# Alternating the row groups of the 32-row inverse products, and splitting a two-bank PSUM tile

## The chip, the cores and the metric

The kernel runs on one core of a Trainium2 chip. The metric is the device time of one launch in microseconds. Five instruction streams run side by side: TensorE (PE, with its weight loads shown apart as PEld), VectorE (DVE), ScalarE (ACT), GpSimd (POOL) and SyncE (SP), which issues DMAs. Each stream is in order, and semaphores join them.

## The reference

One step of a two-layer hybrid decoder over 2064 prompt positions and 8 single-token samples. Each layer projects `x` (1024 channels) to 5128 channels, runs three mixers side by side, projects back and normalises. Two of the mixers matter here.

Retention, per head, runs over the sequence in chunks: scores within the chunk, the old state's contribution, and a new state.

The gated delta rule, per head and chunk of 64 positions, solves a unit lower triangular system and then updates a state:

```
a_low = where(strict, einsum('bhid,bhjd->bhij', kb, k) * decay, 0)
sol   = triangular_solve(eye + a_low, rhs, left_side=True, lower=True)
v_new = u - einsum('bhik,bhkv->bhiv', w, s)
s     = s * exp(g_last) + einsum('bhik,bhiv->bhkv', k * exp(g_last - gc), v_new)
```

The kernel forms the inverse of `eye + a_low` for each chunk and head once, and multiplies by it.

## The kernel before

**Tiling.** Each layer handles the sequence in two halves (`sblock`, 1024 and 1048 columns). A half runs sixteen stages in a written order: keys (K), the RG-LRU heads (A), retention (B) and the delta rule (C). Every stage projects slabs of 128 output channels: `proj` runs 24 matmuls of 128x128 weights on up to 512 columns into a PSUM tile `pj` of one bank. A `Pump` steps generators with the earlier stage's small work between those matmuls.

**The planner.** No engine operation is issued when it is written. `Recorder.note` stores it with its operands; `span` counts PSUM in whole banks over all 128 partitions, so two operations on one bank depend on each other whenever one writes. `places` makes the first users of a pool slot wait for all users of the tile that held it before. `order` then runs a list schedule with fixed costs (a matmul of 32x32 in F32 is put at 0.061 us), taking on each engine, of what is ready, the operation written first; VectorE and ScalarE operations that read PSUM go ahead of others. `issue` emits the operations in that order, and each engine's stream is then fixed; the tile framework adds the semaphores.

**The inverses** (`inverses`). Two chunks of 64 positions lie on partitions 0 to 63 and 64 to 127 of a tile `ap`, for 8 tiles and 4 heads: 32 pairs. Each 64x64 triangle is inverted in 32x32 blocks: `solve` inverts the diagonal blocks on VectorE, and TensorE computes the block below the diagonal, `t21`, by two products of 32x32. They go in two rounds `q` of 16 pairs. The first product (`pg <- tn, ap`) reads rows 0 to 31 for the first chunk and 64 to 95 for the second, and writes partitions 32 to 63 and 96 to 127 of a bank `pg`; VectorE scales it into `gt`, one operation a chunk. The second product (`pg <- tt, gt`) reads rows 32 to 63 and 96 to 127 and writes partitions 0 to 31 and 64 to 95 of another `pg`; ScalarE copies it into `t21`, one copy a chunk. In both products all sixteen of the first chunk come before the sixteen of the second, and in the second product the first chunk's copy is written before the second chunk's products. In the trace a product in F32 shows as two pairs of weight load and matmul. `inverses` runs beside retention or RG-LRU projections, four times in all (two halves, two layers).

**The tile `pz`** is 128 x 1024 F32, two banks, in one slot. In a delta stage (`chain`) four tiles of 128 positions fill it, two tiles to a bank; after them four ScalarE activations and one VectorE multiplication of 64x512 read it into `q.o`. In `retention_bg` the first group of four tiles holds the first bank and the second group the second; `bn_stats` reads each 128 columns as they are finished, and a `tensor_scalar` reads all at the end.

Of the kernel before, what the change touches and what calls it, by code (L numbers as in the profile page):

```python
# [8 lines left out]
F32 = mybir.dt.float32  # L9
F32R = mybir.dt.float32r  # L10
BF = mybir.dt.bfloat16
AF = mybir.ActivationFunctionType
OP = mybir.AluOpType
# [325 lines left out]
def hymba_step(ctx: ExitStack, tc: tile.TileContext, x0t, x0, win, wab, wout, wg, vec, fbc, const, rope,  # L339
# [4 lines left out]
    V, A, PE, G, SP = (Engine(rec, n, e) for n, e in (  # L344
        ("DVE", nc.vector), ("ACT", nc.scalar), ("PE", nc.tensor), ("POOL", nc.gpsimd), ("SP", nc.sync)))
# [5 lines left out]
    psum = Pool(rec, "psum", ctx.enter_context(tc.tile_pool(name="psum", bufs=1, space=PSUM)))  # L351
# [40 lines left out]
    def pt(name="pt"):  # L392
        return psum.tile([128, 512], F32, tag="pt", name=name, bufs=2)
# [2 lines left out]
        return psum.tile([128, 512], F32, tag="pj", name="pj", bufs=2)  # L396

    def pz2():
        return psum.tile([128, 1024], F32, tag="pz", name="pz", bufs=1)

    def p1(tag):
        return psum.tile([128, 512], F32, tag=tag, name=tag, bufs=1)
# [147 lines left out]
    def layer(l):  # L550
# [42 lines left out]
        def sblock(sb):  # L593
# [79 lines left out]
            egw = eg[:, 4].rearrange("p (t h) -> p t h", h=4)  # L673
            egc = eg[:, 0].rearrange("p (t h) -> p t h", h=4)
# [149 lines left out]
            def inverses():  # L824
                nf = nb2.rearrange("p t h -> p (t h)")
                pn = pt("pn")
                PE.transpose(pn[:32, :128], nf[:, :32], ident)
                nbs = small("nbs", [128, 32])
                for c in range(4):
                    A.copy(nbs[32 * c:32 * c + 32], pn[:32, 32 * c:32 * c + 32])  # L830
                a_ = wk.tile([128, 32, 32], F32, tag="q", name="as_", bufs=2)
                apf = ap.rearrange("p t h i -> p i (t h)")
                for c in range(4):
                    o = 32 * (c % 2)
                    V.transpose(out=a_[32 * c:32 * c + 32], in_=apf[32 * c:32 * c + 32, o:o + 32])

                yield
                yield from solve(a_, nbs, t21, tt.rearrange("p s i -> p (s i)"), 128, 32)
                V.transpose(out=tt.rearrange("p s i -> p i s"), in_=t21)
                tn = big("v", "tn")[:, :1024].rearrange("p (s c) -> p s c", c=32)  # L840
                V.transpose(out=tn, in_=tt)
                yield
                yield
                for q in range(2):
                    s = slice(16 * q, 16 * q + 16)
                    pg = pt("pg").rearrange("p (s c) -> p s c", c=32)
                    gt = wk.tile([128, 16, 32], F32, tag="gm2", name="gt", bufs=1)
                    for c in range(2):
                        o = 64 * c
                        for k in range(16):  # L850
                            t, h = divmod(16 * q + k, 4)
                            PE.matmul(pg[o + 32:o + 64, k], ap[o:o + 32, t, h, 32:64], tn[o:o + 32, 16 * q + k],
                                      start=True, stop=True)
                    for c in range(2):
                        o = 64 * c + 32
                        V.tensor_tensor(gt[o:o + 32], pg[o:o + 32],
                                        nf[o:o + 32, s].unsqueeze(2).to_broadcast([32, 16, 32]), op=OP.mult)
                    yield
                    pg = pt("pg").rearrange("p (s c) -> p s c", c=32)
                    for c in range(2):  # L860
                        o = 64 * c + 32
                        for k in range(16):
                            PE.matmul(pg[o - 32:o, k], gt[o:o + 32, k], tt[o:o + 32, 16 * q + k],
                                      start=True, stop=True)
                        A.copy(t21[o - 32:o, s], pg[o - 32:o])
                    yield
                if samp:
                    nbt = small("nbt", [4, 16])
                    pn = pt("pn")
                    PE.transpose(pn[:4, :16], nf[:16, 32:36], ident[:16, :16])  # L870
                    A.copy(nbt, pn[:4, :16])
                    a_ = a_[:, :16]
                    V.transpose(out=a_[:32], in_=apt)
                    t_ = wk.tile([128, 16, 32], F32, tag="gm2", name="gt", bufs=1)
                    G.memset(t_[:32], 0.0)
                    prod = wk.tile([128, 256], F32, tag="gm", name="prod", bufs=2)
                    yield
                    yield from solve(a_, nbt, t_, prod, 4, 16)

                    V.transpose(out=apt, in_=t_[:32])  # L880
# [32 lines left out]
            def delta_bg(h, qT, kT, vT, g):  # L913
# [11 lines left out]
                S = st_g[h]  # L925
# [90 lines left out]

                def chain(q):
                    t4, nt, kk, uv = q.t4, q.nt, q.kk, q.uv
                    q.pz = pz2().rearrange("p (t e c) -> p t e c", t=4, e=2)
                    for i in range(nt):  # L1020
                        for ci, (o, n) in enumerate(((0, 64), (64, 64)) if q.R == 128 else ((0, 16),)):
                            pz = q.pz[:, i, ci]
                            if q.R == 128:
                                PE.matmul(pz, q.wq[:, i, 2 * ci:2 * ci + 2].rearrange("p e c -> p (e c)"), S,
                                          start=True, stop=True)
                            else:
                                PE.matmul(pz[:16], q.wt, S, start=True, stop=True)
                                PE.matmul(q.pz[:16, 0, 1], qT[:, q.c0:q.c0 + 16], S, start=True, stop=True)
                            if q.R == 128:

                                V.tensor_tensor(uv[o:, 1, i], uv[o:, 0, i], pz[o:], op=OP.add)
                            else:
                                V.tensor_tensor(uv[:n, 1, i], uv[:n, 0, i], pz[:n], op=OP.add)
                            yield
                            ps = p1("pd")
                            if q.R == 128:
                                PE.matmul(ps[:, :128], kk[:, 1 - ci, i], uv[:, 1, i], start=True, stop=True)
                            else:
                                PE.matmul(ps[:, :128], kk[:n, 1, i], uv[:n, 1, i], start=True, stop=True)
                            V.scalar_tensor_tensor(out=S, in0=S, scalar=egs[:, ci, t4 + i, h:h + 1],  # L1040
                                                   in1=ps[:, :128], op0=OP.mult, op1=OP.add)
                            yield

                    if q.R == 128:
                        for i in range(nt):
                            A.activation(q.o[64:128, i], q.pz[64:128, i, 0], AF.Copy,
                                         scale=egw[64:128, t4 + i, h:h + 1])
                        V.tensor_tensor(q.o[0:64], q.pz[0:64, :, 1],
                                        egw[0:64, t4:q.t5, h:h + 1].to_broadcast([64, nt, 128]), op=OP.mult)
                    else:  # L1050
                        A.activation(q.o[:16, 0], q.pz[:16, 0, 1], AF.Copy, scale=egc[:16, 8, h:h + 1])

                def outs(q):
                    nt, R = q.nt, q.R
# [192 lines left out]
            def retention_bg(h, qT, kT, vT, g):  # L1247
                S = st_r[h]
# [2 lines left out]
                rs = small("rs", [128, 9])  # L1251
                if samp:
                    G.memset(mv[:, 8], 0.0)
                pz = pz2().rearrange("p (a t c) -> p a t c", a=2, t=4)
                class Group:
                    pass

                def alloc(gi):
                    q = Group()
                    q.t4, q.nt, q.R = tl[gi]  # L1260
                    q.c0 = q.t4 * 128
                    if gi < 2:
                        kv, sn = big(("a1", "a3")[gi], "kv", bufs=1), big(("a2", "a4")[gi], "sn", bufs=1)
                        q.kv, q.sn = (x[:, :1024].rearrange("p (a t c) -> p a t c", a=2, t=4) for x in (kv, sn))
                        q.po = pz[:, gi]
                    else:
                        tk = wk.tile([128, 2, 2, 1, 128], F32, tag="tk", name="tk", bufs=1)
                        q.kv, q.sn = tk[:, 0], tk[:, 1]
                        q.po = p1("po").rearrange("p (t c) -> p t c", t=4)
                    return q  # L1270
# [58 lines left out]
                for q in gs:  # L1329
                    nt, R, c0 = q.nt, q.R, q.c0  # L1330
# [198 lines left out]
        for ri, (r0, R) in enumerate(rows):  # L1529
# [29 lines left out]
            elif last and l + 1 < DEPTH:  # L1559

                ks = [2, 3, 4, 5, 6, 0, 1, 7, 8, 9, 10, 11]
                for i, k in enumerate(ks):
                    for d in range(2):
                        for e, (m_, w_) in enumerate(parts(k)):
                            PE.matmul(ps2[d], m_, w_[:, 512 * d:512 * d + 512], start=(i + e == 0),
                                      stop=(i == 11 and e == 2))
# [5 lines left out]
            else:  # L1572
                for d in range(2):
                    for i, k in enumerate(WO_ORDER):
                        for e, (m_, w_) in enumerate(parts(k)):
                            PE.matmul(ps2[d], m_, w_[:, 512 * d:512 * d + 512], start=(i + e == 0),
                                      stop=(i == 11 and e == 2))
# [212 lines left out]
```

## Time and profile before

| | us |
|---|---|
| median of 3 runs | 3181.75 |
| lowest, highest | 3176.89, 3197.44 |
| the profiled execution | 3189.6 |
| its span, first to last instruction | 3187.8 |
| TensorE busy | 3128.2 |
| VectorE busy | 2050.1 |
| ScalarE busy | 1292.2 |
| GpSimd busy | 676.5 |

Mean granted TensorE clock over the span: 0.987 of full speed (2.4 GHz); a stretch at 0.50 runs at 1.2 GHz. Busy time is the time in which at least one instruction of the engine runs; matmuls overlap, so their durations add up to more than their busy time, and the rate is read from the starts. Names are the program's tiles: `pg<-tn,ap` writes `pg` and reads `tn` and `ap`. Every line is L268, the helper that records operations, so the tile tells which operation it is.

### The profile page before, as it was taken

The numbers are of one execution on the slowest core, as the hardware profiler recorded it, in microseconds if no ns is written. First come the engines' busy times: TensorE is split into PE (matmuls) and PEld (weight loads), VectorE is DVE, ScalarE is ACT, GpSimd is POOL, SyncE is SP. The second block draws the span as 40 slices with busy tenths as digits, with TensorE's granted clock in tenths as the row PEclk, the third lists the DMA queues.
The fourth block names the chain that finished last, engine by engine and source line by source line (L and its number), as shares of the span: only waits on it lengthen the run. The fifth ranks groups of instructions, "written<-read, shape, count | busy, mean of one in ns | idle before, by whom it ended". The sixth has DMA issues, their size and how long they took to land. (4 is left out here: it accounts for less than half of the span.)

```text
span 3187.8 us, 47369 instructions
## 1 busy us (share of the span) xinstructions
PE 3128.2 (98%) x18876; PEld 2745.8 (86%) x18876; DVE 2050.1 (64%) x3704; ACT 1292.2 (41%) x2732; POOL 676.5 (21%) x651
## 2 busy tenths in 40 slices
PE   8999999999999999899999999999999999999999
PEld 6888888899999999788778888888999999997886
DVE  6886565678666565656479655655886665656554
ACT  4445444533454454211144444445334544542100
POOL 2222132222122231111022222222222222311110
PEclk9999999999899999999999999999998999999999
DMA  4111111321111113655321112112211111136541
GB/s 154 62 66 50 55 51 57 111 84 43 42 59 52 49 59 99 190 160 159 116 103 62 51 45 68 50 55 100 84 43 48 54 52 53 55 96 189 169 143 64
DMA packets 137060, 262.97 MB, mean 82 GB/s; under 512 B 24368, under 2 KB 79600, under 8 KB 136840
## 3 DMA queue, kind: packets, MB, share of 16 engines
q1 hardware_dynamic: 113640, 179.91, 17.6%
q0 software_dynamic: 23200, 80.04, 6.9%
q8 instruction: 149, 2.44, 0.3%
q14 instruction: 71, 0.58, 0.1%
HBM read 195.13 MB, written 65.04 MB: 82 GB/s over the span
## 5 line engine op out<-in xcount | busy, mean ns | idle before, releaser
L268 PE MATMUL pj<-arena 128*128 128x512 f32 (+3 forms) x9760 | 2112.0, 361 | 13.7 <-ACT arena L268 8.0
L268 PEld LDWEIGHTS pj<-arena 128*128 128x128 f32 (+1 forms) x9760 | 1631.4, 188 | 168.4 <-ACT arena L268 9.1
L268 POOL TENSOR_TENSOR arena<-raw,arena 128x1024 fp32r<-128x1024 f32 x159 | 401.6, 2526 | 1070.2 <-ACT arena L268 981.8
L268 ACT CAST arena<-raw 128x1024 fp32r<-128x1024 f32 x180 | 188.7, 1048 | 292.7 <-PE pj L268 183.0
L268 DVE SCALAR_TENSOR_TENSOR stg<-stg,eg,pd 128x128 f32<-128x128 f32 x264 | 91.0, 345 | 150.6 <-PE pd L268 148.8
L268 PE MATMUL pj<-arena,ah 128*128 128x512 f32 x512 | 165.3, 402 | 6.7 <-ACT ah L268 6.7
L268 ACT COPY ur<-pj 128x512 f32<-128x512 f32 (+2 forms) x160 | 80.5, 503 | 168.8 <-PE pj L268 168.5
L268 ACT ACT_TABLE_LOAD x106 | 136.0, 1283 | 5.6 <-DVE vT L268 1.9
L268 PEld LDWEIGHTS pj<-arena,ah 128*128 128x128 f32 x512 | 97.4, 191 | 30.3 <-ACT ah L268 7.3
L268 ACT COPY sw<-pj 64x512 f32<-64x512 f32 (+2 forms) x160 | 80.0, 500 | 91.5 <-PE pj L268 51.7
L268 ACT ACTIVATE g<-pj 128x512 f32<-128x512 f32 (+2 forms) x120 | 61.9, 516 | 132.5 <-PE pj L268 131.6
L268 PE MATMUL pj<-arena,al 128*128 128x512 f32 (+1 forms) x296 | 111.6, 398 | 0.2
L268 PE MATMUL pd<-kv 128*128 128x128 f32 x512 | 100.1, 277 | 0.1
L268 PEld LDWEIGHTS pz<-stg,wq 128*128 128x128 f32 x512 | 89.7, 189 | 10.9 <-ACT wq L268 1.6
L268 PE MATMUL pz<-stg,wq 128*128 128x128 f32 x512 | 98.8, 274 | 0.0
L268 ACT ACTIVATE wq<-pz,eg 64x128 f32<-64x128 f32 x128 | 43.3, 360 | 136.0 <-DVE kv L268 88.3
L268 DVE SCALAR_TENSOR_TENSOR g<-g,pj 128x512 f32<-128x512 f32 (+2 forms) x120 | 69.4, 578 | 44.2 <-ACT g L268 43.8
L268 ACT CAST bh<-mb 128x512 fp32r<-128x512 f32 x32 | 19.8, 619 | 189.7 <-PE po L268 107.7
L268 PEld LDWEIGHTS pd<-kv 128*128 128x128 f32 x512 | 86.7, 190 | 10.2 <-issue 1.3
L268 PE MATMUL po<-arena,ah 128*128 128x512 f32 x288 | 92.9, 400 | 0.0
L268 DVE SCALAR_TENSOR_TENSOR qT<-ur,gcw,qT 128x1024 f32<-128x1024 f32 (+1 forms) x48 | 72.2, 1505 | 23.9 <-ACT qT L268 23.6
L268 DVE SCALAR_TENSOR_TENSOR kT<-ur,gcw,kT 128x1024 f32<-128x1024 f32 (+1 forms) x48 | 69.4, 1446 | 21.9 <-ACT kT L268 21.4
(388 smaller groups left out, 5131.7 us busy)
## 6 DMA issues: line engine op xcount, KB each, us to landing
raw<-in_win SPq DMA_DIRECT2D x160, 512.0 KB, 3.2
ma<-mix_d SPq DMA_DIRECT2D x31, 512.0 KB, 5.2
mix_d<-g POOLq DMA_DIRECT2D x24, 520.0 KB, 3.3
mix_d<-g POOLq DMA_DIRECT2D x24, 512.0 KB, 3.1
raw<-in_wout SPq DMA_DIRECT2D x24, 512.0 KB, 3.3
xr<-in_x SPq DMA_DIRECT2D x16, 512.0 KB, 4.7
x_d<-yo POOLq DMA_DIRECT2D x16, 512.0 KB, 3.9
sv<-row_d POOLq DMA_DIRECT2D x16, 512.0 KB, 4.7
```

Source lines behind the costliest of these rows:

```text
L268: return lambda *args, **kw: self._r.note(self._n, op, lambda: f(*args, **kw), args, kw)
```

## The change

In `inverses`, the loop over the two chunks becomes the inner loop of both products, so that a product of the first chunk is followed by the same product of the second. The two copies into `t21` follow after all products. `pz2` returns two tiles of one bank in two slots in place of one tile of two banks; `chain` indexes them by tile (`i // 2`), its multiplication of 64x512 becomes two of 64x256, and `retention_bg` gives one tile to each group.

```diff
     def pz2():
-        return psum.tile([128, 1024], F32, tag="pz", name="pz", bufs=1)
+        return [psum.tile([128, 512], F32, tag="pz", name="pz", bufs=2).rearrange("p (t c) -> p t c", t=4)
+                for _ in range(2)]
...
-                    for c in range(2):
-                        o = 64 * c
-                        for k in range(16):
-                            t, h = divmod(16 * q + k, 4)
+                    for k in range(16):
+                        t, h = divmod(16 * q + k, 4)
+                        for o in (0, 64):
                             PE.matmul(pg[o + 32:o + 64, k], ap[o:o + 32, t, h, 32:64], tn[o:o + 32, 16 * q + k],
                                       start=True, stop=True)
...
-                    for c in range(2):
-                        o = 64 * c + 32
-                        for k in range(16):
+                    for k in range(16):
+                        for o in (32, 96):
                             PE.matmul(pg[o - 32:o, k], gt[o:o + 32, k], tt[o:o + 32, 16 * q + k],
                                       start=True, stop=True)
+                    for o in (32, 96):
                         A.copy(t21[o - 32:o, s], pg[o - 32:o])
...
-                    q.pz = pz2().rearrange("p (t e c) -> p t e c", t=4, e=2)
+                    q.pz = [x.rearrange("p (t e) c -> p t e c", e=2) for x in pz2()]
...
-                            pz = q.pz[:, i, ci]
+                            pz = q.pz[i // 2][:, i % 2, ci]
...
-                        V.tensor_tensor(q.o[0:64], q.pz[0:64, :, 1],
-                                        egw[0:64, t4:q.t5, h:h + 1].to_broadcast([64, nt, 128]), op=OP.mult)
+                        for i in (0, 2):
+                            V.tensor_tensor(q.o[0:64, i:i + 2], q.pz[i // 2][0:64, :, 1],
+                                            egw[0:64, t4 + i:t4 + i + 2, h:h + 1].to_broadcast([64, 2, 128]),
+                                            op=OP.mult)
...
-                pz = pz2().rearrange("p (a t c) -> p a t c", a=2, t=4)
+                pz = pz2()
...
-                        q.po = pz[:, gi]
+                        q.po = pz[gi]
```

## Rows read from the trace of the kernel before

Columns are named with the first group of each view. A timeline row is: start (us), time until the group's last end (us), engine, line, operation, output <- inputs, weights and shape, number of records; in brackets the idle time before it and what ended it. A window row is: the stretch (us), its length, then busy us (and records) of PE, PEld, DVE and ACT (and POOL), the granted clock, the DMA share and GB/s.

**Rows 1.** The page: span; busy time, share and instructions of each engine.

```profile
span 3187.8 us, 47369 instructions
...
PE 3128.2 (98%) x18876; PEld 2745.8 (86%) x18876; DVE 2050.1 (64%) x3704; ACT 1292.2 (41%) x2732; POOL 676.5 (21%) x651
```

**Rows 2.** Timeline of TensorE, first place, 199 to 215 us.

```profile
200.19 2.11 PE L268 MATMUL pg<-tn,ap 32*32 32x32 f32 x64
202.22 1.66 PE L268 MATMUL pj<-arena 128*128 128x512 f32 x6
203.81 1.10 PE L268 MATMUL pg<-tt,gt 32*32 32x32 f32 x29
204.73 0.21 PE L268 MATMUL pg<-tn,ap 32*32 32x32 f32 x1
204.75 0.19 PE L268 MATMUL pg<-tt,gt 32*32 32x32 f32 x1
204.78 0.19 PE L268 MATMUL pg<-tn,ap 32*32 32x32 f32 x1
204.78 0.19 PE L268 MATMUL pg<-tt,gt 32*32 32x32 f32 x1
204.81 0.19 PE L268 MATMUL pg<-tn,ap 32*32 32x32 f32 x1
204.81 0.19 PE L268 MATMUL pg<-tt,gt 32*32 32x32 f32 x1
204.84 1.01 PE L268 MATMUL pg<-tn,ap 32*32 32x32 f32 x28
...
209.17 1.19 PE L268 MATMUL pg<-tt,gt 32*32 32x32 f32 x32
210.29 0.50 PE L268 MATMUL pgt<-ch,wv 128*128 128x512 f32 x1
```

**Rows 3.** Tile pg: min, median, max ns of one; first and last start.

```profile
L268 PE MATMUL pg<-tn,ap x512: 191/191/258, 200.2 to 2412.6; 32*32 32x32 f32 x171
...
L268 DVE TENSOR_TENSOR gt<-pg,nb x16: 683/690/698, 202.3 to 2413.6; 32x512 f32<-32x512 f32 x16
```

**Rows 4.** Windows, tile pg alone, four places: busy by engine, granted clock.

```profile
200.18:212.79 12.61, 8.26 (x256) 7.89 (x256) 2.76 (x4) 1.73 (x3) 1.00 0.12 45
...
sum 76.26, PE 42.23 PEld 40.08 DVE 11.04 ACT 6.92; mean PE 10.56 PEld 10.02 DVE 2.76 ACT 1.73
```

**Rows 5.** Timeline of TensorE, second place, 796 to 830 us.

```profile
802.98 2.11 PE L268 MATMUL pg<-tn,ap 32*32 32x32 f32 x64 [1.30 <-DVE tn L268]
...
815.07 3.43 PE L268 MATMUL pg<-tn,ap 32*32 32x32 f32 x64
```

**Rows 6.** Windows over the same 300 instructions in the first and third place.

```profile
200.18:219.14 18.96, 18.96 (x301) 16.02 (x301) 14.66 (x15) 11.24 (x19) 2.96 (x2) 1.00 0.10 33
1779.07:1803.78 24.71, 24.71 (x301) 20.45 (x301) 12.75 (x15) 11.33 (x19) 2.94 (x2) 0.72 0.09 33
```

**Rows 7.** Windows over the three stretches of lowered clock.

```profile
805.93:822.98 17.05, 17.05 (x173) 15.51 (x172) 2.90 (x5) 4.70 (x10) 2.53 (x2) 0.50 0.09 33
1785.55:1799.19 13.64, 13.64 (x118) 10.79 (x115) 7.13 (x7) 7.79 (x13) 0.00 (x0) 0.50 0.01 1
2399.95:2417.00 17.05, 17.05 (x168) 15.50 (x167) 3.08 (x5) 4.70 (x10) 2.54 (x2) 0.50 0.10 33
```

**Rows 8.** What TensorE waited for: us in total, times, longest.

```profile
PE pz L268 <- DVE bs L268: 5.4, 12, 0.8
```

**Rows 9.** Timeline around one such wait, 848.8 to 851.3 us.

```profile
849.56 0.91 PE L268 MATMUL pz<-kv,sn 128*128 128x128 f32 x6
...
850.51 0.30 DVE L268 BATCH_NORM_STATS2 bs<-pz 128x6 f32<-128x128 f32 x1 [0.58 <-PE pz L268]
...
850.86 0.49 PE L268 MATMUL pz<-kv,sn 128*128 128x128 f32 x2 [0.39 <-DVE bs L268]
```

**Rows 10.** Tile pz: the one read that is split in two.

```profile
L268 DVE TENSOR_TENSOR wq<-pz,eg x32: 681/683/684, 266.0 to 2821.9; 64x512 f32<-64x512 f32 x32
```

More of the change, by code (lines that the diff above doesn't have):

```diff
@@ L1027, in chain @@
                                 PE.matmul(pz[:16], q.wt, S, start=True, stop=True)
-                                PE.matmul(q.pz[:16, 0, 1], qT[:, q.c0:q.c0 + 16], S, start=True, stop=True)
+                                PE.matmul(q.pz[0][:16, 0, 1], qT[:, q.c0:q.c0 + 16], S, start=True, stop=True)
                             if q.R == 128:
@@ L1045, in chain @@
                         for i in range(nt):
-                            A.activation(q.o[64:128, i], q.pz[64:128, i, 0], AF.Copy,
+                            A.activation(q.o[64:128, i], q.pz[i // 2][64:128, i % 2, 0], AF.Copy,
                                          scale=egw[64:128, t4 + i, h:h + 1])
-                        V.tensor_tensor(q.o[0:64], q.pz[0:64, :, 1],
-                                        egw[0:64, t4:q.t5, h:h + 1].to_broadcast([64, nt, 128]), op=OP.mult)
+                        for i in (0, 2):
+                            V.tensor_tensor(q.o[0:64, i:i + 2], q.pz[i // 2][0:64, :, 1],
+                                            egw[0:64, t4 + i:t4 + i + 2, h:h + 1].to_broadcast([64, 2, 128]),
+                                            op=OP.mult)
                     else:
-                        A.activation(q.o[:16, 0], q.pz[:16, 0, 1], AF.Copy, scale=egc[:16, 8, h:h + 1])
+                        A.activation(q.o[:16, 0], q.pz[0][:16, 0, 1], AF.Copy, scale=egc[:16, 8, h:h + 1])
                 def outs(q):
```

## The prediction, made before the changed kernel was run

> **What bounds the kernel now.** I began with the busy times on the page: TensorE is busy 3128.2 of 3187.8 us, every other engine 64% or less [rows 1]. So a change pays here only if it shortens TensorE's own stream or removes one of its waits; work on the other engines counts only where TensorE waits for it. The profiled execution took 3189.6 us, its span plus 1.8; the median of the runs shown is 3181.75.
>
> Next I read the timeline of TensorE where the inverses' products run. There are four such places: two halves of the sequence in each of two layers, starting at 200.2, 803.0, 1779.1 and 2397.2 us. In each, 128 products of 32x32 run, and each product is two load-and-matmul pairs, so 256 records. In the first place 64 records of `tn` fill the stretch from 200.19 to the next projection at 202.22, 2.03 us, 32 ns each [rows 2]. Then comes the row that decides this case: at 204.73 `tn` products on another row group begin while the last `tt` products are still to run, and from 204.73 to 204.84 seven records start, two per 0.03 us. A single row group starts one record per 0.03 us; two together start two. No gap appears when they overlap [rows 2]. The same happens inside the `tn` run, where row group 0 hands over to row group 64.
>
> Then the four places with the granted clock. All `pg` matmuls together take 42.2 us of busy time; in the first place, at clock 1.00, they take 8.26 [rows 4]. In the other three places the clock falls to 0.50, the 1.2 GHz level, for 17.05, 13.64 and 17.05 us [rows 7]. Ahead of the fall in the second place TensorE had stood idle for 1.30 us and then run 2 us of these small products [rows 5]. The first and third place run the same 300 instructions in the same order: 18.96 us with the clock kept, 24.71 with it lowered [rows 6]. That is the price of one fall, 5.75 us for 13.64 us at 0.50, or 0.42 us per us.
>
> Last, TensorE's waits. It waits 12 times for `bs`, 5.4 us in all, before writing `pz` [rows 8]. One such place shows why: the statistics of a tile in one bank of `pz` start only when six records writing the other bank are through, and the next write, again to the other bank, waits for the statistics and costs 0.39 us [rows 9]. The two banks share a tile, and the wait is the tile's.
>
> **The change, part by part.**
>
> **1. Alternating the first product (`tn`), 8 runs of 64 records.** Before: 2.03 us. After, if both row groups keep their own pace, 32 steps of 31.6 ns (64 records in 2.03 us) hold two records each: 1.0 us, and some 0.12 us to the next projection, which the 2.03 already holds for the old order; I take 1.13. Saved 0.9 x 8 = 7.2 us. The pace of sustained alternation is not in the trace, only bursts of about eight records. It is bounded by the burst, 15 ns per record, and by no gain at all, 31.6; a loss is excluded because the overlap shows no pause at a handover. I take the burst, the nearest row: it has the same pair of row groups in the same bank.
>
> **2. Alternating the second product (`tt`).** Before: 16 runs of 32 records, each 1.12 us from its start to the next instruction [rows 2], 2.24 for the two chunks. After: one run of 64 records, 1.13 us. The planner counts a whole bank as one place, so the products of both chunks now form one chain: the first waits for the first scaling of `gt`, the second for the second scaling, 0.69 us later [rows 3]. I expect the first product to go out alone with projections behind it, which adds a small run of some 0.17 us (two steps of 0.03 and 0.1 of handover). Saved (2.24 - 1.13 - 0.17) x 8 = 7.5 us. Behind the waiting product stand the projections, if the planner puts it too early: should VectorE come as late as it does for `tn` in the second place, 1.30 us [rows 5], TensorE would stop for 8 x 1.3 = 10 us at the worst, and for nothing at best. I take nothing, since in the timeline TensorE reaches `tt` 1.6 us after `tn` ends, and two scalings take 1.4. ScalarE's copy of the first chunk now waits for the second chunk's products; nothing on TensorE waits for it for more than the run it joins, and the second chunk's products no longer wait for that copy.
>
> **3. The clock.** With both parts the stretches without large matmuls shrink: 1.30 us idle plus 2.0 of products becomes 1.30 plus 1.1 in the second and fourth place, and in the first and third the runs of `tt` and `tn` that follow each other without a projection [rows 2] halve too. The first place kept its clock through the old runs, so I take the new ones to keep it everywhere. Gain 0.42 x (17.05 + 13.64 + 17.05) = 20.1 us [rows 6, 7]. The bound on the other side is that all three falls stay: no gain here, but parts 1 and 2 then save more, since a record takes 53 ns at the lowered clock (64 in 3.43 us) [rows 5].
>
> **4. One tile becomes two.** The 0.39 us waits on `bs` that cross banks go: ten of them, 3.9 us of the 5.4; the two longer ones (0.8) have another cause, as statistics and write are in one bank there. Bounds 0 and 5.4; I take 4 [rows 8]. The read of 64x512 becomes two of 64x256 in the 32 delta groups; an instruction more each is at most 0.68 us x 32 = 22 us of VectorE [rows 10], hidden while VectorE is 64% busy; with that cover gone it would delay the group's outputs, not TensorE. A delta group's first write no longer waits for the previous group's last read, but TensorE shows no wait on that now, so it is worth nothing. Addresses and DMAs stay as they are; no queue is passed.
>
> **Sum:** 7.2 + 7.5 + 20.1 + 4 = 38.8 us, so 3189.6 - 39 = 3151 against the profiled execution. The median stands 7.9 below the profile; if that is a fall of the clock less, the saving on it is smaller and the end the same; if it is constant, the end is 3143. I say 3149.
>
> **The rivals.**
>
> A. **The clock falls anyway.** Same products, same idle time before them. Then the products save about half of their 42.2 us less the 16 handovers of 0.12, 19 us, and with part 4 the time is 3189.6 - 23 = 3166. For it: three of four places fell, the third with the very sequence that the first survived.
>
> B. **Issue is the limit.** The overlap was fed from records already queued, and a steady stream may be handed out no faster than one per 31.6 ns. Then nothing is gained from parts 1 to 3: 3189.6 - 4 = 3186. Against it: in the overlap the new group's first records came 0.03 us apart while the old ones ran, so the supply kept up at least there. The Trainium skill's page "TensorE: Matmul & The Clock Gate" (Part 1, the section on 56 ns) gives a floor of about 25 ns from start to start, however small the matmul; by that rule parts 1 and 2 would save an estimated 1024 x 6.6 ns = 7 us and the time be 3179. The trace speaks against it: seven starts in 0.11 us.
>
> C. **Slower: row groups exclude each other in one bank.** Both chunks write the same bank of `pg`. If each change of row group let the earlier product finish first, each of the 512 products would wait its 191 ns [rows 3], 98 us in all: 3189.6 + 98 - 4 = 3284. It turns the sign once such a wait exceeds 8 ns (4 us over 512). The Trainium skill's page "TensorEngine Tiling (Array Packing)" (Restrictions and Gotchas, Gotcha 1) says that different row tiles cannot access one PSUM bank simultaneously; that would be this case. The trace against it: inside the `tn` run two row groups hand over in one bank with no pause, as its even 32 ns per record over 2.03 us shows.
>
> D. **Given back.** TensorE runs ahead of a plan that counts these products at their old price, and stops at the second scaling or a later VectorE result: up to 10 us of part 2 lost, and as much again further on, 3170.
>
> **How the numbers follow.** Forecast 0.58, its own range 3139 to 3162; A 0.25; B 0.09; C 0.04; D 0.04. A measurement of this kernel can tell about 1% from no change, that is 32 us: 3150 is the border. Of the forecast I put 0.39 below it and 0.19 above; of A 0.03 below; B and half of D count as no change; C and the other half of D, where the stops cost more than the products save, as slower. Faster 0.42, same 0.52, slower 0.06. The range 3132 to 3176 takes in the forecast and most of A and D, and leaves out B, C and the tails.
>
> **What would show it.** Right: `pg` busy time falls from 42 us to about half; the `tn` runs take 1.1 us; starts come in pairs 31 ns apart; the windows at the four places show clock 1.00; the `bs` waits on `pz` fall to two. Wrong: `tn` runs still of 2 us (B), or of 7 (C); clock 0.50 at the places with short runs (A); new TensorE waits on `gt` (D). Most of the gain hangs on the clock, so the forecast fails first if the clock does not follow the shorter runs.

## The result, and the profile after

The changed kernel takes 3143.39 us in the median of 4 runs (3139.78 to 3149.36), against 3179.32 for the kernel before beside it; the ratio is 0.9879, interval 0.9856 to 0.9902. The forecast of 3149, faster by about 1%, holds in time and sign. By the prediction's own border, 3150, the kernel is faster, to which it gave 0.42, against 0.52 for no change. The profiled execution took 3149.36 us, 40.2 us less than that of before, with a span of 3147.5. The experiments below show that one of the three gains was sized too small and one too large, and that the two errors cancel.

The page of the profile after, span and busy time by engine, answers to [rows 1]:

```profile
span 3147.5 us, 47379 instructions
...
PE 3099.6 (98%) x18876; PEld 2722.0 (86%) x18876; DVE 2047.3 (65%) x3736; ACT 1292.3 (41%) x2732; POOL 674.0 (21%) x651
```

TensorE is 28.6 us less busy and idles 11.7 us less (span less busy time); VectorE runs 32 instructions more, the split reads.

The timeline of TensorE in the first place (start, length, operation, records) answers to [rows 2]:

```profile
198.89 1.20 PE L268 MATMUL pg<-tn,ap 32*32 32x32 f32 x64
200.02 1.66 PE L268 MATMUL pj<-arena 128*128 128x512 f32 x6
201.61 0.24 PE L268 MATMUL pg<-tt,gt 32*32 32x32 f32 x2
201.78 0.73 PE L268 MATMUL pj<-arena 128*128 128x512 f32 x2
202.45 1.10 PE L268 MATMUL pg<-tt,gt 32*32 32x32 f32 x57
...
206.64 0.22 PE L268 MATMUL pg<-tt,gt 32*32 32x32 f32 x2 [0.51 <-DVE gt L268]
...
207.45 1.19 PE L268 MATMUL pg<-tt,gt 32*32 32x32 f32 x62
```

The 64 `tn` records now take 1.13 us to the next projection (198.89 to 200.02), where they took 2.03. The product that goes out ahead of its chain is there, the two records at 201.61 and at 206.64, with two projections behind each; the second of them waits 0.51 us for `gt`.

The windows of the four places, tile `pg` alone (busy us and records by engine, then the granted clock), answer to [rows 4]:

```profile
198.88:208.60 9.72, 4.92 (x256) 4.44 (x256) 2.76 (x4) 1.15 (x2) 1.00 0.16 63
796.44:813.70 17.26, 6.54 (x256) 5.92 (x256) 2.76 (x4) 1.15 (x2) 0.60 0.10 32
1763.00:1772.80 9.80, 4.97 (x256) 4.44 (x256) 2.76 (x4) 1.15 (x2) 1.00 0.16 62
2368.32:2380.40 12.08, 5.04 (x256) 4.48 (x256) 2.76 (x4) 1.16 (x3) 1.00 0.04 7
sum 48.86, PE 21.47 PEld 19.28 DVE 11.05 ACT 4.61; mean PE 5.37 PEld 4.82 DVE 2.76 ACT 1.15
```

Busy time of the products fell from 42.2 to 21.5 us. Three places run at clock 1.00; the second still lost it. Second and fourth place run the same instructions, so two windows over them give the price of a fall once more, as [rows 6] did:

```profile
796.44:821.34 24.90, 24.77 (x341) 22.81 (x342) 11.63 (x25) 10.36 (x19) 5.35 (x6) 0.73 0.14 45
2368.32:2388.01 19.69, 19.11 (x341) 17.81 (x342) 11.63 (x25) 10.24 (x19) 5.39 (x6) 1.00 0.18 56
```

5.21 us for 13.65 us at the lowered clock (798.3 to 812.0), 0.38 us per us; the forecast had 0.42.

What TensorE's matmuls waited for (us in total, times, longest) answers to [rows 8]:

```profile
PE pno L268 <- DVE wq L268: 2.7, 4, 0.7
...
PE pg L268 <- DVE gt L268: 1.6, 3, 0.6
...
PE pz L268 <- DVE str L268: 0.3, 2, 0.2
```

Of the names: `bs` are the statistics of retention, `tk` its small tile for the last group, `str` its state; `wq` holds the output of a delta group, and `pno` the transpose of it; `qk` are scores, `pgt` the gates of RG-LRU. No wait of `pz` on `bs` or `tk` is left, where two on `bs` were expected to stay. The 6.2 us of `pno` on `wq` became 2.7, which the prediction did not speak of, and 1.6 us on `gt` are new.

### The profile page after: what moved, and what is told of

Read it like the earlier page. It is cut to its first block, busy times and chain, and to the rows that moved or that the text cites. A ratio compares the mean times of both kernels' runs of the same rounds, so it can differ in the third digit from the quotient of the medians.

```text
span 3147.5 us, 47379 instructions
## 1 busy us (share of the span) xinstructions
PE 3099.6 (98%) x18876; PEld 2722.0 (86%) x18876; DVE 2047.3 (65%) x3736; ACT 1292.3 (41%) x2732; POOL 674.0 (21%) x651
## 5 line engine op out<-in xcount | busy, mean ns | idle before, releaser
L268 DVE TENSOR_TENSOR kv<-kv,pz 128x128 f32<-128x128 f32 (+1 forms) x128 | 37.0, 289 | 78.8 <-PE pz L268 78.4
```

The source lines that it names most:

```text
L268: return lambda *args, **kw: self._r.note(self._n, op, lambda: f(*args, **kw), args, kw)
```

## The experiments

Each run lists its mean granted clock, so the time at the lowered level is 2 x (1 - clock) x span. Over the 96 runs of all ten kernels, one line with a slope in common fits: time = (the kernel's own time) + 0.41 x (time at the lowered clock), and leaves 2 us of scatter. So the kernels are compared twice below: as measured, and at equal clock, which takes 0.41 us off for each us at the lowered level. The runs of before are the 37 that ran beside the experiments; each ratio goes by those beside it, that of the changed kernel by the four named above.

| kernel | runs | median us | ratio to before (interval) | mean us at lowered clock | against before at equal clock |
|---|---|---|---|---|---|
| before | 37 | 3184 | | 76 | |
| after | 4 | 3143.39 | 0.9879 (0.9856 to 0.9902) | 44 | -28 |
| alternation alone | 6 | 3159.55 | 0.9915 (0.9897 to 0.9934) | 41 | -12 |
| split tile alone | 9 | 3170.78 | 0.9954 (0.9935 to 0.9972) | 74 | -14 |
| two smaller reads alone | 12 | 3184.09 | 0.9990 (0.9976 to 1.0005) | 82 | -4 |
| runs cut, old order | 12 | 3197.04 | 1.0036 (1.0018 to 1.0054) | 94 | +4 |
| after, chunks reversed in the second product | 5 | 3143.05 | 0.9865 (0.9841 to 0.9888) | 49 | -31 |
| the same, later in the plan | 5 | 3143.44 | 0.9872 (0.9855 to 0.9889) | 44 | -28 |
| after, four row groups in turn | 5 | 3145.61 | 0.9879 (0.9862 to 0.9897) | 40 | -25 |

The tenth kernel, the blocks, ran once, for its trace. The last column has a standard error of some 1 us; differences of 2 or 3 us in it are within what so few runs can tell.

**Alternation alone.** The two loops of the change, on the old tile `pz`.

```diff
 def pz2():
     return psum.tile([128, 1024], F32, tag="pz", name="pz", bufs=1)
...
-for c in range(2):
-    for k in range(16): ...
+for k in range(16):
+    for o in (0, 64): ...
```

> Only the alternation of the two chunks; the tile pz stays one tile of two banks. Theory (three separate gains: products 15 us, clock 15 to 20, split tile 4 to 9): 30 to 35 us under the kernel before, about 3147; pg records start 16 ns apart, the waits of TensorE on bs stay at about 5 us and those of pno on wq at about 6. Rival (the gain is mostly a luckier order of the whole plan that the split tile brought): no more than 15 us, the products' own saving, about 3164.

Measured 0.9915, which is 27 us of 3184 (21 to 33 by the interval). The records start 16 ns apart, and no place lost its clock in the profile. The waits of the matmuls (us, times, longest):

```profile
PE pno L268 <- DVE wq L268: 6.3, 4, 1.6
...
PE pz L268 <- DVE bs L268: 4.2, 12, 0.4
...
PE pg L268 <- DVE gt L268: 2.2, 4, 0.6
```

The waits of the old tile are all there. 27 us lie between the theory's 30 to 35 and the rival's 15, nearer the theory. At equal clock 12 us remain for the products, against the 14.7 forecast; the new wait on `gt`, 2.2 us, is most of the difference. And 35 us less at the lowered clock are worth 0.41 x 35 = 14.

**The split tile alone.** The change with both loops put back to the old order.

```diff
-for k in range(16):
-    for o in (0, 64): ...
+for c in range(2):
+    for k in range(16): ...
```

> Only the split of the tile pz; the products in the old order of chunks. Theory: 4 us by the prediction, up to 9 by the waits that the changed kernel has lost (bs 5.4, tk 0.8, half of pno's wait on wq), so 3170 to 3175; three falls of the clock at the inverses stay, at least in the profile. Rival (order luck): 20 us or more, 3160 or less.

Measured 0.9954, 14 us at equal clock, three times the forecast's 4. The time lies in the theory's range, though the gain is above its 9, as the kernel before took 3184 beside it; the rival's 20 is not reached. Of the three falls of the clock that were expected to stay, two did, in the second and the fourth place; the third place kept its clock. The prediction counted one wait of the matmuls; all their waits together fell by 9.9 us (50.9 to 41.0). More is seen on the stream of weight loads, whose short stops lie under the end of the matmul before. Waits of the weight loads, kernel before:

```profile
PEld pno L268 <- DVE wq L268: 7.9, 4, 2.0
PEld pz L268 <- DVE bs L268: 7.7, 12, 1.0
...
PEld pz L268 <- ACT wq L268: 3.1, 16, 0.3
...
PEld pz L268 <- DVE tk L268: 1.2, 2, 0.6
```

and with the split tile alone:

```profile
PEld pno L268 <- DVE wq L268: 4.4, 4, 1.1
...
PEld pz L268 <- DVE str L268: 1.5, 2, 0.8
...
PEld pz L268 <- issue: 1.2, 8, 0.2
```

`bs` 7.7, `ACT wq` 3.1 and `tk` 1.2 are gone, and `pno` lost 3.5: 15.5 us, less 1.5 of a new wait on `str` and 1.2 at eight of the sixteen places of `ACT wq`, which now show as `issue`. All weight-load waits together fell from 120.9 to 105.8 us in the two traces, 15.1 us, close to the gain. By the code the sixteen waits on `ACT wq` are a group's first writes, into the first bank, behind the activations of the group before, the last of which read the second bank.

**Two smaller reads alone.** The kernel before with the multiplication of 64x512 cut in two, on the old tile.

```diff
-V.tensor_tensor(q.o[0:64], q.pz[0:64, :, 1], ..., op=OP.mult)
+for i in (0, 2):
+    V.tensor_tensor(q.o[0:64, i:i + 2], q.pz[0:64, i:i + 2, 1], ..., op=OP.mult)
```

> The kernel before with one part of the change: the read of 64x512 becomes two of 64x256, on the old tile of two banks; products in the old order. Theory (the split tile pays because waits were counted for the whole tile): 12 waits on bs and 16 waits of the weight loads on wq stay, and the time stays within 4 us of before, 3180 to 3188. Rival (the smaller reads let the delta groups end earlier and that is the gain): the wait of pno on wq falls from 6.2 to 2.7 us, and 5 to 10 us are gained.

Neither is right alone. Waits of the weight loads:

```profile
PEld pz L268 <- DVE bs L268: 5.4, 8, 1.0
...
PEld pno L268 <- DVE wq L268: 4.4, 4, 1.1
...
PEld pz L268 <- issue: 2.5, 12, 0.3
...
PEld pz L268 <- DVE str L268: 1.3, 4, 0.3
...
PEld pz L268 <- DVE tk L268: 1.2, 2, 0.6
PEld pz L268 <- DVE wq L268: 1.1, 4, 0.3
```

The `pno` wait falls to 4.4 as the rival said (2.7 on the matmuls). The waits of `pz` change their names more than their sum: four on `bs` and the 16 on `ACT wq` are gone, and `issue`, `str` and `DVE wq` stand in their place, 11.5 us in all against 12.0 before and 2.7 with the split tile. The time moved by 0.1%, within the noise, 4 us at equal clock. So of the 14 us of the split some 4 belong to the smaller reads (the wait of `pno`) and 10 to the tile's own boundary (the waits of `pz`), if the two add.

**Runs cut, old order.** Kernel before, the first product in pieces of 8 with a PSUM tile and a scaling each.

```diff
+for k0 in (0, 8):
+    pg = pt("pg").rearrange("p (s c) -> p s c", c=32)
-    for k in range(16):
+    for k in range(k0, k0 + 8):
         PE.matmul(pg[o + 32:o + 64, k], ap[...], tn[o:o + 32, 16 * q + k], start=True, stop=True)
+    V.tensor_tensor(gt[o + 32:o + 64, k0:k0 + 8], pg[...], nf[...], op=OP.mult)
```

> The kernel before with the old order of chunks, but the first product cut into four pieces of 8 products with a PSUM tile and a scaling each, so that the long runs of 64 records break into runs of 16 to 32 with projections between. Each record still takes its 32 ns. Theory (falls of the clock follow the long runs and cost 0.42 us per us): fewer falls at the inverses, 6 to 20 us under the kernel before, about 3166, with pg busy time as before at full clock (33 us). Rival (the falls follow the amount of small products, not the length of the run): the falls stay and the time stays within 5 us of before.

Both fail: the kernel is slower. All four places lose the clock, and for longer, 91.9 us in these windows (the column after POOL is the granted clock) where it was 47.7 [rows 7]:

```profile
207.65:224.70 17.05, 17.05 (x139) 13.21 (x137) 6.68 (x8) 7.47 (x12) 2.34 (x1) 0.50 0.10 33
815.20:842.40 27.20, 27.20 (x245) 23.98 (x244) 4.36 (x15) 6.75 (x16) 3.57 (x4) 0.50 0.06 20
1798.30:1818.70 20.40, 20.40 (x148) 15.82 (x146) 7.29 (x9) 9.66 (x15) 2.34 (x1) 0.50 0.08 27
2416.10:2443.30 27.20, 27.20 (x245) 23.98 (x244) 4.33 (x15) 6.75 (x15) 3.57 (x4) 0.50 0.06 20
```

Short runs between projections do not keep the clock here: the same small products, spread over a longer stretch, had it lowered for longer. Which place falls is not settled by one profile. With the two smaller reads alone, whose products run in the old order, the first place lost its clock too, and the fourth, which runs the order of the second, kept it:

```profile
203.70:217.30 13.60, 13.60 (x185) 11.14 (x182) 7.97 (x8) 7.61 (x13) 0.00 (x0) 0.62 0.01 2
2404.60:2418.20 13.60, 13.60 (x233) 12.35 (x232) 2.63 (x4) 5.61 (x12) 3.00 (x3) 1.00 0.12 41
```

The mean over the 12 runs stands more firmly, 94 us against 76. The price is the same: 18 us more at the lowered clock in the mean is 7 us, and 4 more come at equal clock, out of 12 measured.

**Chunks reversed in the second product.** The changed kernel, so that the chain waits for both scalings before its first product.

```diff
-for o in (32, 96):
+for o in (96, 32):
     PE.matmul(pg[o - 32:o, k], gt[o:o + 32, k], tt[o:o + 32, 16 * q + k], start=True, stop=True)
```

> The changed kernel with the second product's chunks in the order second, first, so that the chain starts only when both scalings are done. Theory (the single product that goes out ahead costs two handovers and sometimes a wait of 0.5 us on gt): the lone runs of 2 records disappear, no wait on gt, 2 to 3 us under the changed kernel, about 3141. Rival (projections fill that time at no cost): no difference.

The runs of two records are gone; the timeline of the second place (wait and releaser in brackets):

```profile
793.19 1.20 PE L268 MATMUL pg<-tn,ap 32*32 32x32 f32 x64 [1.29 <-DVE tn L268]
...
797.03 1.20 PE L268 MATMUL pg<-tt,gt 32*32 32x32 f32 x64 [0.51 <-DVE gt L268]
...
800.19 1.20 PE L268 MATMUL pg<-tn,ap 32*32 32x32 f32 x64
...
803.75 1.20 PE L268 MATMUL pg<-tt,gt 32*32 32x32 f32 x64
```

The wait on `gt`, expected to go, stays and grows from 1.6 to 2.4 us in all, four times. At equal clock the kernel is 3 us below the changed one, as expected, but its clock was lowered for 5 us more; the medians, 3143.05 and 3143.39, do not differ. It is the lowest of all, by less than can be told.

**The same, later in the plan.** Five more steps of the generator ahead of the first product.

```diff
 V.transpose(out=tn, in_=tt)
 yield
 yield
+yield   # five times
```

> The kernel with the reversed order of chunks in the second product, and five more steps of the generator before the first product, so that the second and fourth place come later in the plan: TensorE no longer waits 1.3 us for tn, and more projections lie between the runs. Theory (a fall comes from the density of small products and idle time over a stretch): no falls at the four places in any run, the 2.6 us of waits on tn and the 2.4 on gt gone, 3 to 6 us under the kernel with the reversed order, about 3138. Rival (the later inverses delay the delta stage behind them): as much is lost there, no difference.

No place lost its clock in the profile. The waits on `tn` fall from 2.6 to 0.9 us, but those on `gt` rise from 2.4 to 2.8, that of `pno` on `sn` from 1.8 to 3.1, and one of `pj` on `g` is new:

```profile
PE pno L268 <- ACT sn L268: 3.1, 2, 2.3
PE pg L268 <- DVE gt L268: 2.8, 6, 0.7
PE pj L268 <- DVE g L268: 2.8, 2, 1.4
```

The median, 3143.44, is that of the kernel without the steps: the rival's outcome.

**Blocks.** Chunks reversed as above; the first product alternates in blocks of 8 in round 0 and of 4 in round 1.

```diff
-for k in range(16):
-    for o in (0, 64): ...
+n = (8, 4)[q]
+for k0 in range(0, 16, n):
+    for o in (0, 64):
+        for k in range(k0, k0 + n): ...
```

> The changed kernel with reversed order of chunks in the second product; the first product alternates in blocks of 8 products a chunk in round 0 and of 4 in round 1. Theory (each row group holds about four records ready, so a new group starts four records before the old one ends): 24 ns per record with blocks of 8 (64 records in 1.5 us), 16 ns with blocks of 4. Rival A (supply looks ahead as far as it needs): 16 ns with both. Rival B (only strict alternation overlaps): 28 to 31 ns with both.

Windows over a run with blocks of 8 and one with blocks of 4, tile `pg` (length, busy us, records):

```profile
198.75:200.68 1.93, 1.85 (x64) 1.79 (x64) 0.00 (x0) 0.00 (x0) 1.00 0.09 30
807.90:809.42 1.52, 1.47 (x64) 1.36 (x64) 0.01 (x1) 0.00 (x0) 1.00 0.00 0
```

From first to last start they take 1.72 and 1.32 us, 27 and 21 ns a record, between the theory and rival B. Start to last start is 1.92 us with one handover (before), 1.72 with three, 1.32 with seven: each handover takes 0.1 us off, three records at 31.6 ns. So a row group runs ahead by about three records, not four, and of the orders that were run only strict alternation overlaps throughout (1.01 us).

**Four row groups in turn.** Second product of round 0 and first of round 1 in one loop.

```diff
+for k in range(16):
+    second(p1_, gt, 0, k)     # rows 96 and 32
+    first(p2, 1, k)           # rows 0 and 64
+copies(p1_, 0)
+gt = scaled(p2, 1)
...
```

> The changed kernel, but the second product of round 0 and the first of round 1 alternate too, so that all four row groups take turns (in the order of two each); the second product's chunks in the order second, first. Theory (each row group takes one record per 31.6 ns, whatever the others do): the 128 records of this stretch start 8 ns apart and take 1.0 us instead of 2.0, 4 x 1 us saved, about 3139. Rival (some supply common to all limits the stream to about the 16 ns that two groups reach): the stretch stays at 2 us and the time at that of the kernel with the reversed order of chunks, 3143.

Two windows over these 128 records, tile `pg`:

```profile
203.90:205.20 1.30, 1.21 (x128) 1.17 (x128) 0.00 (x0) 0.00 (x0) 1.00 0.78 315
802.45:803.70 1.25, 1.21 (x128) 1.18 (x128) 0.00 (x0) 0.00 (x0) 1.00 0.00 0
```

They take 1.09 us from first to last start, 8.6 ns a record with the start of the run and 8 once it is under way: the theory's pace, and there is no limit at the rival's 16 ns. Yet the kernel is no faster than the changed one, 3145.61. The matmuls' waits show where it went; together they are 48.2 us, against 40.4 with the reversed order alone:

```profile
PE qk L268 <- ACT wq L268: 5.5, 6, 0.9
...
PE pgt L268 <- ACT wv L268: 3.8, 2, 3.2
PE pgt L268 <- DVE gt L268: 3.0, 2, 1.5
PE pno L268 <- ACT sn L268: 2.9, 2, 2.0
```

After the change `pgt` did not wait on `gt` at all and 0.6 us on `wv`, `pno` waited 1.7 on `sn` and `qk` 3.6. One of these waits can be followed in the first place:

```profile
207.51 1.39 DVE L268 TENSOR_TENSOR gt<-pg,nb 32x512 f32<-32x512 f32 x2
...
209.05 0.47 PE L268 MATMUL pgt<-ch,wv 128*128 128x512 f32 x1 [1.50 <-DVE gt L268]
```

`pg` and `pgt` are tiles of one pool with two slots. The joint loop fills two `pg` at once, so `pgt` has no slot until the scalings, which end at 208.90, have read one of them. That TensorE comes earlier to results that VectorE and ScalarE deliver no sooner may hold for the other waits, but was not followed.

## Why the prediction was right, step by step

**Parts 1 and 2, the products: right in mechanism, nearly in size.** Two row groups take turns at 16 ns a record for as long as the run lasts, as the burst of seven starts had shown [rows 2]. Forecast 14.7 us; at equal clock the alternation alone gave 12, and with the single product ahead of the chain removed perhaps 3 more. That product was foreseen, at 0.17 us each, for eight chains, and went out at six; the wait on `gt`, 0.5 us where it occurs, was foreseen as a bound and taken as nothing.

**Part 3, the clock: the term was too large.** Forecast 20.1 us. The price per us holds (0.42 forecast, 0.38 and 0.41 measured). So does the direction: with the old order the four kernels spent 74 to 94 us in the mean at the lowered clock, with alternation the five in the table 40 to 49. But the second place still lost its clock in the profile, and there was more time at the lowered clock elsewhere: outside the four places some 35 us before (83 in all less 47.7) and 43 after (57 less 13.7), by the mean granted clocks, which are given to about 3 us. In the profile that makes 0.41 x 26 = 11 us, in the means of all runs 0.41 x 32 = 13. The step that failed is "I take the new ones to keep it everywhere". Its ground, that shorter runs keep the clock, is no rule: with the first product's runs cut, and no run of small products above 1.5 us at full clock where the changed kernel has 2.0, the clock fell at all four places.

**Part 4, the split tile: the term was too small.** Forecast 4 us, bounds 0 and 5.4; measured 14. The row it rested on counts one wait of the matmuls, `bs`. Their waits of `pz` on `tk` (0.8 us) and of `pno` on `wq` (3.5 of 6.2) went too, and the weight loads, whose stops are longer, lost 15.1 us of waits. The bound of 5.4 was wrong, since it assumed that TensorE showed no other wait that hangs on this tile and its reads; the statement that a group's first write waiting for the last read was worth nothing failed with it, as the 3.1 us of weight-load waits on `ACT wq` show.

**The sum.** 15 + 20 + 4 was forecast, 12 + 13 + 14 was measured: 39 both times. The mechanisms of all three parts are there, but that the sum came out is luck: the split tile gave 10 us more than forecast, the clock 7 and the products 3 less. The forecast had two ends, 3151 for the profiled execution and 3143 for the median if the distance between the two held; they came at 3149.36 and 3143.39. The 3149 that was stated lies between, 6 us above the median.

**The rivals.** A, the clock falls anyway: it happened at one place of four in the profile, at none with alternation alone; elsewhere in the program falls remain in every profile. B, a limit of issue: excluded by 16 ns over whole runs and 8 ns with four groups. The floor of 25 ns from start to start in the Trainium skill ("TensorE: Matmul & The Clock Gate", Part 1) does not bind here. C, row groups exclude each other in one bank: excluded by the same 16 ns, as both groups write one `pg`. The rule of the Trainium skill's "TensorEngine Tiling (Array Packing)" (Restrictions and Gotchas, Gotcha 1) does not show as a loss of time where the two row groups write different partitions of the bank. D, given back: 1.6 us on `gt` here; with four groups the whole further gain went into waits.

What stays open is what makes the clock fall: the experiments give its price and show that the length of a run alone does not decide it; at the same order of instructions it falls at one place and not at another. That alternation halves the time in small products and that less time at the lowered clock goes with it is shown; why is not.

## What to carry to other kernels

Small products on different row groups of TensorE should take turns one by one: a row group that runs alone sets the pace, and blocks overlap only at their seams. A PSUM tile of two banks made the users of one bank wait for those of the other here; give each bank its own tile, and count the slots of a pool before an order that fills two tiles at once. Count the stops of TensorE on its weight loads as well as on its matmuls, and price a lowered clock by the same instructions at both levels.

## What the runs showed of the hardware

- A row group took one record (weight load and matmul of 32x32 F32) per 31.6 ns whatever the others did: 31.6 ns a start with one group, 16.0 with two, 8 with four (8.6 over all 128 records).
- A group that follows another ran about three records ahead of its end: 0.1 us saved per handover. A stream is issued in order, but the starts of two row groups then mix: from 204.73 to 204.81 us single `tn` and `tt` records take turns, though a product's two records are issued one behind the other [rows 2].
- At the 1.2 GHz level the same records started 26.7 ns apart with two groups (kernel after, second place, the `tn` run at 806.6 us) and 54 with one (kernel before, the `tt` runs of the second place).
- Time at the lowered clock cost 0.41 us per us over 96 runs, less than the 0.5 that a stretch bound by TensorE alone would give.
